# Where the operands of the matrix products lie in SBUF: moved by part of 512 bytes, by role

## The chip, the core and the metric

The kernel runs on one core of a Trainium2 chip. The metric is the device time of one execution in microseconds (us). TensorE (PE) multiplies a stationary operand, loaded beforehand by a weight load (PEld), with a moving operand that streams through it; VectorE (DVE), ScalarE (ACT) and GpSimd (POOL) work on tiles in SBUF, and SyncE (SP) and GpSimd issue DMAs. SBUF has 128 partitions; a tile takes the same byte range in each, and an address below is the byte in a partition.

## What is computed

Two layers of an encoder on 512 tokens of 1024 features, in float32. Layer 0 mixes tokens by neighbourhood attention on an 8 x 64 grid, layer 1 by three dilated windowed attentions that are merged by their softmax denominators. Each layer ends in a gated feed-forward part with 2816 hidden features.

```
for layer in range(2):
    h = rms_norm(x, norm_mix_pre[layer])
    h = neighbourhood_attention(h, ...) if layer == 0 else dilated_attention(h, ...)
    x = x + rms_norm(h, norm_mix_post[layer])
    h = rms_norm(x, norm_ffn_pre[layer])
    x = x + rms_norm(swiglu(h, w_gate, w_up, w_down), norm_ffn_post[layer])
swiglu(x) = (silu(x @ w_gate) * (x @ w_up)) @ w_down
```

## The kernel before

**How a product is made.** Each float32 operand is split into a high part `h` and a low part `l`, both in float32r, by ACT (line 365) and DVE (line 366). `mm3` (lines 377 to 379) makes one product as three matmuls: h by h, h by l, l by h. In its calls `s` is stationary (128 columns are loaded as weights) and `m` is moving (256 or 512 columns). A trace row such as `gu<-rxa,h_c` names the output in PSUM, then both operands; in these rows the moving operand stands first, except that one name stands alone when both lie in the same tile.

**Seven products for eight.** A unit of class `Seven` makes a 2 by 2 block product with seven products of 12 `mm3` matmuls each (84 in all), from sums of weights and sums of activations: p1, p2, d1, s2, s4, s3, x2b. Gate and up of one block of 128 hidden features make one unit, so `gate_up` runs 22 units a layer (output `gu`), with the first products of three units ahead. Query and key of a pair of heads make one unit too: 8 in layer 0 (output `pp_n`), 24 in layer 1 (`pp_d`). `Values` does the same for the values of layer 1 (`vd`), with the activations stationary and the weights moving. In all of these the moving operand has 256 columns.

**Where the operands lie.** The ring of weights is the pool `wpool`: eight tiles `h_*` and `l_*` of 4096 bytes, turned over by the split. Activations lie in `rxa` (ten parts of D = 1024), `rxc` (five parts and a bit) and `rxb` (an arena that is opened for the mixers). The weights of the product s4 go to a ring of two slots: `vmem` and the last part of `rxc` (layer 0's mixer: the last part of `ao`). So in gate/up the moving operands are X1A and X1B in `rxc` and D1, S2, S4, S3, X2B in `rxa`; in the mixers X1A, X1B, X2B and D1 are in `rxa` and S2, S4, S3 in `rxb`.

**512 columns.** `down` turns the roles round: the hidden activations are split into a ring `hl_` of five parts of `rxc` and are stationary, the weights from the ring `wpool` are moving with 512 columns (outputs `yd_s`, `yd_pp`). `out_proj` (output `yo`) has the attention's result in `rxa` stationary and moves the output weights, which are split into two ring tiles, `wm` and `vmem`, the last part of `rxa`, and `rxb`.

**Order.** Class `Order` simulates the instructions on five engines with fixed costs and pins each engine's order. Its costs do not depend on SBUF addresses, but which instruction waits for which does depend on what overlaps in a tile.

**Places.** The allocator puts the tiles of `cpool` one behind the other, then `wpool`, then the arenas. Parts are whole multiples of 512 bytes, so every operand of a tile has its tile's residue modulo 512, but for score operands with an extra 64 columns (256 bytes).

Of the kernel before, what the change touches and what calls it, by code (L numbers as in the profile page):

```python
# [13 lines left out]
F32 = mybir.dt.float32  # L14
F32R = mybir.dt.float32r
# [15 lines left out]
EPS = 1e-6  # L31
MEM, ARENA = 14544, 9 * D
NEG = -1e30
BIG = 3.0e38
X1A, X1B, X2B, D1, S2, S4, S3 = range(7)
BANKS = {"pp": 3, "s": 2, "t": 2, "o": 1}
SLOPES = [float(np.float32(2.0) ** np.float32(-8.0 * (h + 1) / HEADS)) for h in range(HEADS)]
# [259 lines left out]
def encoder_kernel(ctx: ExitStack, tc: tile.TileContext, a: dict, out: bass.AP):  # L297
# [3 lines left out]
    cpool = ctx.enter_context(tc.tile_pool(name="cpool", bufs=1))  # L301
    wpool = ctx.enter_context(tc.tile_pool(name="wpool", bufs=4))
    psum = ctx.enter_context(tc.tile_pool(name="psum", bufs=1, space=bass.MemoryType.PSUM))
    dpool = ctx.enter_context(tc.tile_pool(name="dpool", bufs=1, space=bass.MemoryType.DRAM))

    ident = cpool.tile([P, P], F32, name="ident")
    make_identity(nc, ident)
    mhalf = cpool.tile([P, 1], F32, name="mhalf")
    dve.memset(mhalf, -0.5)
    spill = [dpool.tile([NT, P, D], F32, name=f"spill{i}") for i in range(3)]  # L310
# [12 lines left out]
    rxa = cpool.tile([P, 10 * D], F32R, name="rxa")  # L323
    rxc = cpool.tile([P, 5 * D + 256], F32R, name="rxc")
    vmem = cpool.tile([P, D], F32R, name="vmem")

    mem = cpool.tile([P, MEM], F32, name="mem")
    rvd = [dpool.tile([PAIRS, P, D], F32, name=f"rvd{i}") for i in range(2)]
# [18 lines left out]
    def w22_ring(mem):  # L347
        return cycle([hl(vmem, 0, 512), hl(mem, 0, 512)])

    small_ = cycle(range(20))  # L350

    def small(name, n=1):
        if "o0" in name or "o1" in name:
            return tagged(cpool, [P, n], F32, f"small_o{next(small_)}", name, 1)
        return tagged(cpool, [P, n], F32, f"small{n}", name, 16 if n > 1 else 12)
# [463 lines left out]
    def gate_up(layer, xs, hid, more, rings, sums):  # L819
        wg, wu = a["wg"], a["wu"]  # L820
        raws = ring(more, 0, 2 * D, 3)
        g_, u_, p5_ = rings
        v_ = w22_ring(rxc[:, 4 * D:5 * D])
        units, us = {}, {}
# [186 lines left out]
    def hl(mem, i, n):  # L1011
        return mem[:, i * D:i * D + n], mem[:, i * D + n:i * D + 2 * n]
# [24 lines left out]
    def mix_out(layer, w, rxb, wm, load_x):  # L1037
        for j in range(PAIRS - 1):
            nc.gpsimd.dma_start(rxa[:, j * D:(j + 1) * D], rvd[layer][j])

        us = [None] * 2 + [hl(wm, 0, D), (wm[:, 2 * D:], vmem), hl(rxa, 8, D)] + [hl(rxb, 2 * i, D) for i in range(3)]

        out_proj(w, rv, layer, load_x, us, (ring(mem, 4 * D, D, 4), ring(mem, 0, D, 4), ring(mem, 13440, 512, 2)),
                 (mem[:, 11392:11392 + D], mem[:, 12416:12416 + D]))

    def ffn(layer, stack, memc):
        hl_ = ring(rxc, 0, D, 5)
        rxb = None
# [98 lines left out]
    inner.close()  # L1147
    with arena("wm0", 3 * D, "right", F32R) as wm:
        mix_out(0, a["na_o"], rxb, wm, lambda xt, t: nc.sync.dma_start(xt, a["x_rows"][t]))
# [13 lines left out]
    p5_ = ring(memc, 2560, 256, 2)  # L1163
    q_, k_, kl_, ost_ = rxc[:, 0:D], rxc[:, D:2 * D], rxc[:, 2 * D:3 * D], ring(rxc, 3 * D, D, 1)
    w22_ = w22_ring(rxc[:, 4 * D:5 * D])
    def by_token(v):
# [192 lines left out]

    vus, vslots = {}, cycle([hl(rxc, 0, D), hl(rxc, 2, D), (vmem, rxc[:, 4 * D:5 * D])])  # L1360
    for qd in range(2):
# [67 lines left out]
    inner.close()  # L1429
    with arena("wm1", 3 * D, "right", F32R) as wm:  # L1430
        mix_out(1, a["dil_o"], rxb, wm, load_block)
# [92 lines left out]
```

## Time and profile before

| | us |
|---|---|
| three runs: median (lowest to highest) | 1484.54 (1484.52 to 1489.98) |
| the profiled execution | 1487.69 |
| its span, from the first to the last instruction | 1485.9 |

A window of the trace gives the busy time of each engine in a stretch of the span. The stages lie about so (us from the span's start): layer 0's mixer to 205, its output projection to 264, gate/up to 490, down to 597; layer 1's values to 735, its queries, keys and attention to 1070, the output projection to 1144, gate/up to 1376, down to 1478. Matmuls overlap in the pipeline, and the duration of one is modelled; the distance from one start to the next is measured, and is what to read of a stream of them. A weight load starts some 3 ns behind the matmul ahead of its own.

### The profile page before, as it was taken

How to read it: one execution, taken by the hardware profiler on the slowest of the kernel's cores; microseconds unless marked ns; L12 is line 12 of the kernel's file. 1: busy time of each engine (PE TensorE's matmuls, PEld its weight loads, DVE VectorE, ACT ScalarE, POOL GpSimd, SP SyncE). 2: the span in 40 equal slices, each digit the busy share in tenths (PEclk: the TensorE clock that was granted, in tenths of full speed). 3: DMA queues.
4: the chain of work that ended last, by engine and by line, in shares of the span. 5: the costliest groups of instructions: out<-in, count | busy, mean ns of one | idle time of the engine just before them, and what ended most of it. 6: DMA issues, size and time to landing. Idle time of an engine off the chain costs nothing.

```text
span 1485.9 us, 27934 instructions
## 1 busy us (share of the span) xinstructions
PE 1442.8 (97%) x10788; PEld 1333.1 (90%) x10788; DVE 1196.8 (81%) x1876; ACT 904.1 (61%) x1819; POOL 542.4 (37%) x398
## 2 busy tenths in 40 slices
PE   7999999899999999999999999999999999999997
PEld 6988877899999888899999999989977999999886
DVE  5499967699889788797689788787657989998877
ACT  4478874555555567544467778876675654555664
POOL 5345425544231001665555444334204644330001
PEclk9999999899999999999999999999999999999999
DMA  5346487677333664435433343333766788834662
GB/s 200 139 177 179 155 286 206 227 221 212 114 112 114 204 220 162 168 126 187 142 100 101 93 145 116 100 133 103 237 206 214 200 243 243 252 126 149 203 208 92
DMA packets 86645, 253.22 MB, mean 170 GB/s; under 512 B 19312, under 2 KB 31600, under 8 KB 84464
## 3 DMA queue, kind: packets, MB, share of 16 engines
q1 hardware_dynamic: 77696, 197.69, 40.4%
q0 software_dynamic: 8672, 53.48, 13.9%
q8 instruction: 85, 1.39, 0.4%
q14 instruction: 48, 0.39, 0.1%
q10 hardware_dynamic: 144, 0.26, 0.0%
HBM read 229.24 MB, written 68.29 MB: 200 GB/s over the span
## 4 chain that ended last, share of the span: by engine, by line
PE 77%; DVE 8%; ACT 7%; DMA 3%; issue 3%; POOL 1%; SPq 0%; POOLq 0%; DVEq 0%; ACTq 0%
PE gu L377 10%; PE gu L378 9%; PE gu L379 9%; PE pp_d L377 5%; PE pp_d L379 4%; PE pp_d L378 4%; PE yd_s L377 3%; PE yd_s L379 3%; PE yd_s L378 3%; PE yd_pp L377 2%; PE yd_pp L379 2%; PE yd_pp L378 2%; PE sb L1274 2%; PE yo L377 2%; PE yo L379 1%
## 5 line engine op out<-in xcount | busy, mean ns | idle before, releaser
L585 POOL TENSOR_TENSOR rs_yd<-v_yd,mhalf 128x1 f32<-128x1 f32 x8 | 8.3, 1043 | 261.3 <-DVE v_yd L583 261.3
L378 PE MATMUL gu<-rxa,h_b 128*128 128x256 f32 x352 | 100.0, 284 | 2.5 <-DVE rxa L602 2.5
L377 PE MATMUL gu<-rxc,h_a 128*128 128x256 f32 x352 | 99.7, 285 | 2.0 <-ACT h_a L365 1.2
L377 PE MATMUL gu<-rxa,h_c 128*128 128x256 f32 x352 | 99.7, 283 | 1.3 <-DVE memc L839 1.1
L378 PE MATMUL gu<-rxc,h_a 128*128 128x256 f32 x352 | 99.7, 284 | 1.2 <-DVE rxc L602 1.0
L377 PE MATMUL gu<-rxa,h_b 128*128 128x256 f32 x352 | 99.7, 284 | 1.2 <-ACT rxa L601 1.2
L379 PE MATMUL gu<-rxa,l_b 128*128 128x256 f32 x352 | 99.6, 283 | 0.2 <-DVE l_b L366 0.2
L379 PE MATMUL gu<-rxc,l_a 128*128 128x256 f32 x352 | 99.1, 282 | 0.0
L378 PE MATMUL gu<-rxa,h_c 128*128 128x256 f32 x352 | 98.7, 280 | 0.0
L379 PE MATMUL gu<-rxa,l_c 128*128 128x256 f32 x352 | 98.3, 280 | 0.0
L365 ACT ACTIVATE rxc<-mem 128x512 fp32r<-128x512 f32 (+2 forms) x90 | 55.9, 624 | 65.9 <-PE yd_pp L378 33.8
L445 POOL TENSOR_TENSOR r_d<-r_d 128x512 f32<-128x512 f32 x24 | 36.1, 1506 | 161.0 <-DVE l_ad L366 122.9
L445 POOL TENSOR_TENSOR r_gu<-r_gu 128x512 f32<-128x512 f32 x20 | 30.6, 1529 | 149.8 <-DVE l_a L366 102.4
L366 DVE TENSOR_TENSOR rxc<-mem,rxc 128x512 fp32r<-128x512 f32 (+2 forms) x90 | 64.4, 719 | 19.5 <-ACT rxc L365 19.2
L445 POOL TENSOR_TENSOR raw<-raw 128x512 f32<-128x512 f32 x24 | 38.0, 1582 | 99.4 <-DVE l_a L366 74.7
L378 PEld LDWEIGHTS gu<-rxa,h_b 128*128 128x128 f32 x352 | 67.6, 192 | 2.7 <-DVE rxa L602 2.7
L377 PEld LDWEIGHTS gu<-rxc,h_a 128*128 128x128 f32 x352 | 67.1, 192 | 2.8 <-ACT h_a L365 1.4
L377 PEld LDWEIGHTS gu<-rxa,h_c 128*128 128x128 f32 x352 | 66.5, 189 | 2.9 <-DVE memc L839 1.3
L378 PEld LDWEIGHTS gu<-rxc,h_a 128*128 128x128 f32 x352 | 67.2, 191 | 1.8 <-DVE rxc L602 1.8
L377 PEld LDWEIGHTS gu<-rxa,h_b 128*128 128x128 f32 x352 | 67.3, 192 | 1.5 <-ACT rxa L601 1.4
L1238 ACT ACTIVATE mem<-mem 128x256 f32<-128x256 f32 x128 | 63.8, 504 | 7.5 <-DVE mem L1237 7.3
L379 PEld LDWEIGHTS gu<-rxa,l_b 128*128 128x128 f32 x352 | 67.4, 191 | 0.4 <-DVE l_b L366 0.4
(610 smaller groups left out, 6157.7 us busy)
## 6 DMA issues: line engine op xcount, KB each, us to landing
wsum<-wd POOLq DMA_DIRECT2D x24, 1408.0 KB, 12.1
r_d<-dil_qk SPq DMA_DIRECT2D x48, 512.0 KB, 4.1
raw<-wg SPq DMA_DIRECT2D x24, 512.0 KB, 5.1
raw<-wu SPq DMA_DIRECT2D x24, 512.0 KB, 8.4
wsum<-wsum POOLq DMA_DIRECT2D x8, 1408.0 KB, 10.3
raw<-wsum SPq DMA_DIRECT2D x22, 512.0 KB, 4.3
r_gu<-wg SPq DMA_DIRECT2D x20, 512.0 KB, 3.8
r_gu<-wu SPq DMA_DIRECT2D x20, 512.0 KB, 4.9
```

Of the source, the lines that this page charges most:

```text
L365: act.activation(h, src, AF.Copy)
L366: dve.tensor_sub(l, src, h.bitcast(F32))
L377: i = pe.matmul(o, s[0], m[0], start=start, stop=False, skip_group_check=True)
L378: pe.matmul(o, s[0], m[1], start=False, stop=False, skip_group_check=True)
L379: pe.matmul(o, s[1], m[0], start=False, stop=stop, skip_group_check=True)
L445: self.added = e[0].tensor_add(q[0], q[0], q[2])
L585: pool.tensor_tensor(r, v, mhalf, op=ALU.pow)
L1238: act.activation(pr[:, f], pr[:, f], AF.Exp, bias=st[:, c:c + 1], scale=-1.0, accum_out=st[:, c + 2:c + 3])
L1274: pe.matmul(ss[hd][:, f0:f0 + P], qf[rw, block(c)], kf[rw, block(c)], start=True, stop=True)
```

## The change

It shifts tiles so that residues modulo 512 differ or agree by role. `ident` and `mhalf` change places, `mem` comes ahead of `vmem`, the twenty small tiles `small_o*` become columns of one tile `few_small`, a pad of 48 floats ends the last pool ahead of the arenas, `wm` is 80 floats longer, and five parts of `rxc` are taken from 80 floats (320 bytes) on, as `rxs`: the `hl_` ring of `down`, the s4 slot, and in layer 1 the keys, the result's ring and the slots of `Values`. X1A and X1B of gate/up and the queries stay at `rxc`'s start. `rxb`, which is allocated behind the pad, starts at another residue.

In the built programs the residues are:

| tile | before | after |
|---|---|---|
| `rxa`, `rxc`, `mem` | 160 | 160 |
| `rxs`, the shifted parts of `rxc` | 160 (unshifted) | 480 |
| `vmem` | 160 | 480 |
| ring of weights `h_*`, `l_*` | 480 | 480 |
| `rxb`, the weights' raw arena | 480 | 160 |
| `wm` | 480 | 160 |
| `memc`, `akl`, `ao` | 480 | 480 |
| `ident` | 128 | 160 |

Of the 8,056 float32r matmuls with 256 moving columns, 1,760 have both operands at one residue before and 48 after; of the 1,308 with 512 columns, 64 before and 1,196 after.

No instruction is added or removed. The order is the same on all engines but at the end of layer 0's gate/up and the start of its down, where the first parts of the `hl_` ring now overlap two of gate/up's operands in `rxc`. On DVE, there, the low parts of down's first activations (`rxc<-mem`) and those of the last units' weights (`l_b`, `l_c`; `r_gu` and `raw` are weights as loaded) stood before as:

```order
L366 TENSOR_TENSOR rxc<-mem,rxc 128x512
L366 TENSOR_TENSOR l_b_19_5179<-raw_2880,h_b_19_5178 128x1024
L841 TENSOR_TENSOR memc_2876<-mem,gu_18_4749 128x256
L366 TENSOR_TENSOR l_c_19_5238<-raw_2880,h_c_19_5237 128x1024
L845 TENSOR_TENSOR mem<-memc_2876,mem 128x2x256
L366 TENSOR_TENSOR l_b_20_5260<-r_gu_20_4977,h_b_20_5259 128x1024
L836 TENSOR_TENSOR memc_2876<-memc_2876,gu_21_5096 128x256
L366 TENSOR_TENSOR l_c_20_5319<-r_gu_20_4977,h_c_20_5318 128x1024
L435 MEMSET gu_21_5096 128x256
L845 TENSOR_TENSOR mem<-memc_2876 128x2x256
L366 TENSOR_TENSOR rxc<-mem,rxc 128x512 x3
```

and stand now as:

```order
L373 TENSOR_TENSOR l_b_19_5156<-raw_2857,h_b_19_5155 128x1024
L852 TENSOR_TENSOR mem<-memc_2853,mem 128x2x256
L848 TENSOR_TENSOR memc_2853<-mem,gu_18_4726 128x256
L373 TENSOR_TENSOR l_c_19_5215<-raw_2857,h_c_19_5214 128x1024
L373 TENSOR_TENSOR rxc<-mem,rxc 128x512 x2
L373 TENSOR_TENSOR l_b_20_5237<-r_gu_20_4954,h_b_20_5236 128x1024
L843 TENSOR_TENSOR memc_2853<-memc_2853,gu_21_5073 128x256
L373 TENSOR_TENSOR l_c_20_5296<-r_gu_20_4954,h_c_20_5295 128x1024
L442 MEMSET gu_21_5073 128x256
L852 TENSOR_TENSOR mem<-memc_2853 128x2x256
L373 TENSOR_TENSOR rxc<-mem,rxc 128x512
```

One split of down's activations stood ahead of the four splits of gate/up's weights, and three behind them; now two stand in their middle, and the next ones behind. On PE, at the same place, the products of units 20 and 21 (`gu_20`, `gu_21`) and the first of down (`yd_pp`) stood before as:

```order
L379 MATMUL gu_20_4980<-rxa,l_c_20_5319 128x256
L377 MATMUL gu_20_4980<-rxa,h_c_20_5318 128x256
L378 MATMUL gu_20_4980<-rxa,h_c_20_5318 128x256
L379 MATMUL gu_20_4980<-rxa,l_c_20_5319 128x256
L377 MATMUL gu_21_5096<-rxa,rxc 128x256
L378 MATMUL gu_21_5096<-rxa,rxc 128x256
L379 MATMUL gu_21_5096<-rxa,rxc 128x256
L377 MATMUL gu_21_5096<-rxa,rxc 128x256
```

and stand now as:

```order
L385 MATMUL gu_20_4957<-rxa,h_c_20_5295 128x256
L386 MATMUL gu_20_4957<-rxa,l_c_20_5296 128x256
L385 MATMUL gu_21_5073<-rxa,h_b_21_5317 128x256
L386 MATMUL gu_21_5073<-rxa,l_b_21_5318 128x256
L384 MATMUL yd_pp_5410<-h_d0p_0_5415,rxc 128x512
L385 MATMUL yd_pp_5410<-l_d0p_0_5416,rxc 128x512
L384 MATMUL gu_20_4957<-rxa,h_c_20_5295 128x256
L385 MATMUL gu_20_4957<-rxa,h_c_20_5295 128x256
```

Between two dozens of matmuls of unit 20 stood six of unit 21's s4; now two of its product before and two of down's first stand there, and the six come later. Names end in running numbers, which differ in the two programs by a constant.

The diff:

```diff
@@ -29,10 +29,11 @@
 COLS = 64
 ROWS = 8
 EPS = 1e-6
-MEM, ARENA = 14544, 9 * D
+MEM, ARENA = 14544, 9 * D + 80
 NEG = -1e30
 BIG = 3.0e38
 X1A, X1B, X2B, D1, S2, S4, S3 = range(7)
+SHIFT = 80
 BANKS = {"pp": 3, "s": 2, "t": 2, "o": 1}
 SLOPES = [float(np.float32(2.0) ** np.float32(-8.0 * (h + 1) / HEADS)) for h in range(HEADS)]
 
@@ -300,13 +301,13 @@
 
     cpool = ctx.enter_context(tc.tile_pool(name="cpool", bufs=1))
     wpool = ctx.enter_context(tc.tile_pool(name="wpool", bufs=4))
+    zpool = ctx.enter_context(tc.tile_pool(name="zpool", bufs=1))
     psum = ctx.enter_context(tc.tile_pool(name="psum", bufs=1, space=bass.MemoryType.PSUM))
     dpool = ctx.enter_context(tc.tile_pool(name="dpool", bufs=1, space=bass.MemoryType.DRAM))
 
+    mhalf = cpool.tile([P, 1], F32, name="mhalf")
     ident = cpool.tile([P, P], F32, name="ident")
     make_identity(nc, ident)
-    mhalf = cpool.tile([P, 1], F32, name="mhalf")
-    dve.memset(mhalf, -0.5)
     spill = [dpool.tile([NT, P, D], F32, name=f"spill{i}") for i in range(3)]
 
     tags, arenas, extra = {}, [], []
@@ -322,9 +323,15 @@
 
     rxa = cpool.tile([P, 10 * D], F32R, name="rxa")
     rxc = cpool.tile([P, 5 * D + 256], F32R, name="rxc")
+
+    mem = cpool.tile([P, MEM], F32, name="mem")
     vmem = cpool.tile([P, D], F32R, name="vmem")
 
-    mem = cpool.tile([P, MEM], F32, name="mem")
+    few_small = cpool.tile([P, 32], F32, name="few_small")
+    pad = zpool.tile([P, 48], F32, name="pad")
+    dve.memset(mhalf, -0.5)
+
+    rxs = rxc[:, SHIFT:SHIFT + 5 * D]
     rvd = [dpool.tile([PAIRS, P, D], F32, name=f"rvd{i}") for i in range(2)]
 
     tops = {"left": 0, "right": 0}
@@ -347,11 +354,11 @@
     def w22_ring(mem):
         return cycle([hl(vmem, 0, 512), hl(mem, 0, 512)])
 
-    small_ = cycle(range(20))
+    small_ = cycle([few_small[:, i:i + 1] for i in range(20)])
 
     def small(name, n=1):
         if "o0" in name or "o1" in name:
-            return tagged(cpool, [P, n], F32, f"small_o{next(small_)}", name, 1)
+            return next(small_)
         return tagged(cpool, [P, n], F32, f"small{n}", name, 16 if n > 1 else 12)
 
     def load2(srcs, name, raw=None):
@@ -820,7 +827,7 @@
         wg, wu = a["wg"], a["wu"]
         raws = ring(more, 0, 2 * D, 3)
         g_, u_, p5_ = rings
-        v_ = w22_ring(rxc[:, 4 * D:5 * D])
+        v_ = w22_ring(rxs[:, 4 * D:])
         units, us = {}, {}
 
         def unit_of(f):
@@ -1038,13 +1045,13 @@
         for j in range(PAIRS - 1):
             nc.gpsimd.dma_start(rxa[:, j * D:(j + 1) * D], rvd[layer][j])
 
-        us = [None] * 2 + [hl(wm, 0, D), (wm[:, 2 * D:], vmem), hl(rxa, 8, D)] + [hl(rxb, 2 * i, D) for i in range(3)]
+        us = [None] * 2 + [hl(wm, 0, D), (wm[:, 2 * D:3 * D], vmem), hl(rxa, 8, D)] + [hl(rxb, 2 * i, D) for i in range(3)]
 
         out_proj(w, rv, layer, load_x, us, (ring(mem, 4 * D, D, 4), ring(mem, 0, D, 4), ring(mem, 13440, 512, 2)),
                  (mem[:, 11392:11392 + D], mem[:, 12416:12416 + D]))
 
     def ffn(layer, stack, memc):
-        hl_ = ring(rxc, 0, D, 5)
+        hl_ = ring(rxs, 0, D, 5)
         rxb = None
         hm = mem[:, :FT * 512]
         h2 = hm.rearrange("p (h x) -> p h x", h=2)
@@ -1145,7 +1152,7 @@
              lambda v: v.rearrange("p (i c) -> p i c", i=ROWS))
 
     inner.close()
-    with arena("wm0", 3 * D, "right", F32R) as wm:
+    with arena("wm0", 3 * D + 80, "right", F32R) as wm:
         mix_out(0, a["na_o"], rxb, wm, lambda xt, t: nc.sync.dma_start(xt, a["x_rows"][t]))
     stack.close()
     memc = inner.enter_context(arena("memc0", 3 * D, "right"))
@@ -1161,8 +1168,8 @@
     pt_, few_ = ring(ap, 10 * D, D, 4), ring(mem, 0, 96, 2)
     bt, qs, ks = memc[:, 0:1536].rearrange("p (k c) -> p k c", c=P), memc[:, 1536:2048], memc[:, 2048:2560]
     p5_ = ring(memc, 2560, 256, 2)
-    q_, k_, kl_, ost_ = rxc[:, 0:D], rxc[:, D:2 * D], rxc[:, 2 * D:3 * D], ring(rxc, 3 * D, D, 1)
-    w22_ = w22_ring(rxc[:, 4 * D:5 * D])
+    q_, k_, kl_, ost_ = rxc[:, 0:D], rxs[:, D:2 * D], rxs[:, 2 * D:3 * D], ring(rxs, 3 * D, D, 1)
+    w22_ = w22_ring(rxs[:, 4 * D:])
     def by_token(v):
 
         return v.rearrange("p (m r) -> p r m", r=4)
@@ -1357,7 +1364,7 @@
     order = [3 * j + g for j in range(PAIRS) for g in orders[j]]
     stats, parts, weight, pts, vg, ready, left, later = {}, {}, {}, {}, {}, [], {}, {}
 
-    vus, vslots = {}, cycle([hl(rxc, 0, D), hl(rxc, 2, D), (vmem, rxc[:, 4 * D:5 * D])])
+    vus, vslots = {}, cycle([hl(rxs, 0, D), hl(rxs, 2, D), (vmem, rxs[:, 4 * D:])])
     for qd in range(2):
         v = v_quarter(ap[:, (6 + qd) * D:(7 + qd) * D], a["dil_v"][0, qd], f"d{qd}")
         nc.sync.dma_start(vd[0][qd].rearrange("t p c -> p t c"), v)
@@ -1427,7 +1434,7 @@
                 nc.sync.dma_start(xt[32 * r + 16:32 * r + 32], rows[r, 0:16])
 
     inner.close()
-    with arena("wm1", 3 * D, "right", F32R) as wm:
+    with arena("wm1", 3 * D + 80, "right", F32R) as wm:
         mix_out(1, a["dil_o"], rxb, wm, load_block)
     stack.close()
     memc = inner.enter_context(arena("memc1", 3 * D, "right"))
```

## The prediction

> **What bounds the kernel now.** I read the page first, then windows by stage, then the timeline of TensorE alone. The page:
>
> ```profile
> span 1485.9 us, 27934 instructions
> ...
> PE 1442.8 (97%) x10788; PEld 1333.1 (90%) x10788; DVE 1196.8 (81%) x1876; ACT 904.1 (61%) x1819; POOL 542.4 (37%) x398
> ...
> PE 77%; DVE 8%; ACT 7%; DMA 3%; issue 3%; POOL 1%; SPq 0%; POOLq 0%; DVEq 0%; ACTq 0%
> ```
>
> TensorE makes 77% of the chain that ended last. The windows (stretch and its length; busy time and count of PE, PEld, DVE, ACT, POOL; granted clock; DMA share; GB/s) say where it never rests:
>
> ```profile
> 300.00:425.00 125.00, 125.00 (x1063) 125.00 (x1062) 114.75 (x138) 65.64 (x113) 48.62 (x32) 1.00 0.60 176
> 490.00:597.00 107.00, 107.00 (x483) 88.31 (x482) 92.44 (x124) 68.93 (x108) 7.00 (x4) 1.00 0.61 197
> 735.00:1070.00 335.00, 330.77 (x2837) 310.45 (x2837) 262.62 (x551) 243.65 (x619) 141.30 (x93) 1.00 0.40 122
> 1175.00:1345.00 170.00, 168.69 (x1427) 168.06 (x1426) 155.43 (x189) 87.23 (x152) 66.62 (x45) 1.00 0.76 214
> 1376.00:1478.00 102.00, 101.74 (x437) 82.06 (x435) 82.79 (x112) 61.38 (x96) 3.02 (x3) 1.00 0.54 171
> ```
>
> Gate/up (rows 1 and 4) and down (rows 2 and 5) have PE busy for nearly all their length at a granted clock of 1.00: there the time is the number of matmuls times the distance from one start to the next. Gate/up is 1063 in 125.00 us (117.6 ns each) and 1427 in 168.69 us (118.2 ns). So the question is whether places change that distance. The timeline has starts to 10 ns, so I divide long runs (first column start, second modelled duration):
>
> ```profile
> 299.78 0.28 PE L378 MATMUL gu<-rxa,h_c 128*128 128x256 f32 x1
> ...
> 305.11 0.28 PE L378 MATMUL gu<-rxc,h_a 128*128 128x256 f32 x1
> 305.22 0.28 PE L377 MATMUL gu<-rxa,vmem 128*128 128x256 f32 x1
> ...
> 306.54 0.28 PE L379 MATMUL gu<-rxa,vmem 128*128 128x256 f32 x1
> 306.65 0.28 PE L379 MATMUL gu<-rxc,l_a 128*128 128x256 f32 x1
> ...
> 312.66 0.28 PE L379 MATMUL gu<-rxc,l_a 128*128 128x256 f32 x1
> ```
>
> This is the key view. From 299.78 to 305.11 lie 47 steps: 113.4 ns each; moving operand at 160 modulo 512 bytes, weights from the ring at 480. From 305.22 to 306.54, 11 steps with weights in vmem at 160, the same residue as the moving operand: 120.0 ns. From 306.65 to 312.66 the weights are in the ring again, yet 51 steps take 117.8 ns each. So there are **three paces of 256 columns**: 120 when the places agree, and for places apart a fast one (113.4) and a slow one (117.8). Before the agreeing run the pace is fast, behind it slow, and it stays slow through the rest of the stretch. Is it the place, or vmem?
>
> ```profile
> 737.72 0.28 PE L378 MATMUL pp_d<-rxb,vmem 128*128 128x256 f32 x1
> ...
> 738.89 0.28 PE L379 MATMUL pp_d<-rxb,vmem 128*128 128x256 f32 x1
> 742.66 0.28 PE L378 MATMUL pp_d<-rxb,h_cd 128*128 128x256 f32 x1
> ...
> 743.38 0.28 PE L378 MATMUL pp_d<-rxb,h_cd 128*128 128x256 f32 x1
> ```
>
> With the moving operand in rxb at 480, vmem is apart: 10 steps in 1.17 us, 117. And there the ring, itself at 480, gives 120 (6 steps in 0.72). The place it is.
>
> **The change part by part.** It adds no instruction and removes none but names; all it does to the time must come through these paces, or through waits.
>
> ```profile
> L378 PE MATMUL gu<-rxa,h_b 128*128 128x256 f32 x352 | 100.0, 284 | 2.5 <-DVE rxa L602 2.5
> L378 PE MATMUL gu<-rxa,vmem 128*128 128x256 f32 x88 | 24.9, 283 | 0.0
> L377 PE MATMUL pp_d<-rxb,h_cd 128*128 128x256 f32 x96 | 27.8, 290 | 0.7 <-DVE mem L683 0.7
> ```
>
> *Gate/up, 256 columns.* 9 groups like the first row (x352) and 6 like the second (x88) are 3,696 matmuls, 528 of them on agreeing places, one group of 12 in each unit of 84. After the change all are apart. Direct gain: 528 x (120.0 - 117.8) = 1.2 us. The larger one: nothing throws the fast pace out any more. If all of the 1063 + 1427 ran at 113.4, that is 125.00 + 168.69 - 2490 x 0.1134 = 11.3 us; the other 1,206, in stretches broken by waits and partly fast already, I put at 2 us: at most 13.3. Not all will be fast, since a wait can end in either pace:
>
> ```profile
> 1347.76 0.39 PE L377 MATMUL gu<-rxa,h_c 128*128 128x256 f32 x1
> 1347.99 0.28 PE L378 MATMUL gu<-rxa,h_c 128*128 128x256 f32 x1
> ...
> 1349.04 0.28 PE L378 MATMUL gu<-rxa,h_c 128*128 128x256 f32 x1
> ```
>
> Here a disturbed start (one step of about 0.23 us) is followed by 9 steps in 1.05 us, 117: slow, with no agreeing place near; the stretch above at 299.78 came out of its wait fast. Of the 50 stretches of eight steps or more that begin behind a wait with these two residues, the first at 80 us and the last at 1372, the timeline has 34 at the fast pace. I take three quarters, since the one at 299.78 would have run on for a third of the layer. A quarter at the slow pace gives back 0.25 x 3,696 x 4.4 ns = 4.1 us: **-9.3 us**, bounds 0 (all slow) and -13.3.
>
> What hides it: DVE is busy 114.75 of 125.00 us in the first row of windows. At the fast pace that stretch lasts 120.5; DVE would fill 95% of it. It still fits, barely, which is a reason not to count on all of it.
>
> *Query/key products of both mixers.* 6 groups like the third row have rxb against the ring, 576 agreeing, and layer 0's 8 units 24 each the same way, with 48 more in ao; afterwards apart. 816 x (120 - 115, between both paces) = 4.1 us, but PE has gaps there (330.77 of 335) and transposes and scores disturb it in every unit: I keep half, **-2.0**, bounds 0 and -5.
>
> *Value products and scores of layer 1.* Here the change makes moving 480, stationary 160, apart the other way round. The nearest rows, vmem above at 117, have that order at the slow pace. 5 units of 7 products of 24 matmuls are 840, over half of them apart already: **+0.5**, bounds -2 and +2.
>
> *Down and output projection, 512 columns.* Down was apart (160 and 480) and becomes equal:
>
> ```profile
> 521.55 0.39 PE L377 MATMUL yd_pp<-h_d0d,rxc 128*128 128x512 f32 x1
> ...
> 577.86 0.39 PE L377 MATMUL yd_s<-h_d0s,rxc 128*128 128x512 f32 x1
> 1400.58 0.40 PE L377 MATMUL yd_pp<-h_d1d,rxc 128*128 128x512 f32 x1
> ...
> 1457.98 0.40 PE L377 MATMUL yd_s<-h_d1s,rxc 128*128 128x512 f32 x1
> 227.78 0.39 PE L377 MATMUL yo<-rxa 128*128 128x512 f32 x1
> 228.46 0.63 PE L377 MATMUL yo<-rxb,rxa 128*128 128x512 f32 x2
> 248.88 0.40 PE L377 MATMUL yo<-rxa 128*128 128x512 f32 x1
> ...
> 250.27 0.40 PE L377 MATMUL yo<-rxb,rxa 128*128 128x512 f32 x1
> ```
>
> 246 steps each: 228.9 ns in layer 0, 233.3 in layer 1: two paces again, for one and the same code. Equal places exist before only in yo with both operands in rxa: 3 steps in 0.68 us, 226.7, the shortest seen; another such group has 6 in 1.39, 231.7. Two of the eight short groups reach 226.7. Over 924 matmuls of down that is -4.1 us if both layers catch the short pace, +0.5 if neither does. By the count of groups I take **-1.0**; yo's own 224 that become equal stand beside waits: 0, bounds +-1.
>
> *The rest.* small_o values in one tile: the same instructions wait for the same engines; 0. Transposes keep their form with ident 32 bytes further; the nearest price is the 6.6 ns between agreeing and fast at 256 columns, on some 340: 0, bounds 0 and +2. The moved order at the end of layer 0's gate/up is one slot of operands later on DVE, where PE sat busy from 425 on; 0, bounds +-1.
>
> Sum: -9.3 - 2.0 + 0.5 - 1.0 = **-11.8 us**. The profiled execution took 1487.69 us (span 1485.9 and 1.8 around it), so 1475.9 in its place. It is 3.15 over the median of the three runs (1484.54), of which layer 1's slow pace in down may be 437 x 4.4 ns = 1.9 us; from the median the sum gives 1472.7.
>
> A rule speaks against the change: the Trainium skill, "TensorE: Matmul & The Clock Gate", section "Step-by-step: what each phase is for", says that TensorE has two independent read ports and that loading the next weights takes no read bandwidth from the running matmul. By it places would be without effect. The rows at 305.22 and 742.66 disagree, at 120.0 against 113.4. The same page, "Wait — 56ns, not 53.3ns?", puts a step at columns over 2.4 GHz plus about 2.5 ns, an estimate of 109.2 for 256; no steady stretch here is below 113.
>
> **The rivals.**
> 1. *The slow pace sticks.* Every stretch of gate/up drops to 117.8 whatever the places. For it: long stretches are slow now, and the wait at 1347.76 ends slow. Against: 47 steps at 113.4 without a break. Time: the direct gains alone, -1.2 and some -1 in the mixers, and +0.5 for the values: about 1483.
> 2. *Places have no effect*, and the paces come from tiles or the state of the engine: 1484.5. Against it the two views of vmem.
> 3. *DVE becomes the bound of gate/up, and it gets slower than before.* The place is the splits of weights beside GpSimd's sums. DVE has 125.00 - 114.75 = 10.3 us free over some 12.6 units, 0.8 us a unit. A faster PE shifts which sums meet on their shared SBUF path; from 0.8 us more collision a unit on, PE waits in every unit, and each such wait may drop the pace too. At 1 us more a unit, 44 units x 0.2 = 9 us: 1493. Against it: no instruction is added, and the wait would hold PE back again, which undoes the shift.
> 4. *All goes fast*, gate/up whole and down at 226.7: -13.3 - 4.1 - 2.0 + 0.5 = -18.9: 1465.6.
>
> **How the numbers follow.** Forecast 0.50; rival 4 0.17; rival 1 0.20; rival 2 0.08; rival 3 0.05. Half a per cent, about what a measurement of this kernel can tell from no change, is 7.4 us: below 1477.1 counts as faster. Forecast (mostly) and rival 4 are faster: 0.67. Rivals 1, 2 and a little of the forecast are within: 0.29. Rival 3: 0.04. The range from 1464 to 1484 leaves out about half of rivals 2 and 4, and rival 3.
>
> **What would show it.** Gate/up's x84 a unit in 9.5 us instead of 9.9; no 120 ns stretch behind vmem or rxc; whole units at 113 between waits; the two downs at one of 226.7 or about 231. Wrong would be: gate/up at 117.8 throughout (rival 1), waits for DVE before gu in every unit (rival 3), down above 233.

## The result, and the profile after

| | before | after |
|---|---|---|
| time, us, median (range) of 7 runs each, beside each other | 1489.98 (1484.52 to 1493.61) | 1478.99 (1475.11 to 1480.66) |
| profiled execution, us | 1487.69 | 1480.66 |
| ratio of times | 1 | 0.9933, 95% interval 0.9915 to 0.9950 |

The kernel became faster by 0.67%, beyond the half per cent that can be told from no change. The seven runs of before have a higher median than the three shown ahead of the prediction. From the page of the changed kernel, the span, the busy times and the engines of the chain that ended last:

```profile
span 1478.8 us, 27934 instructions
...
PE 1433.6 (97%) x10788; PEld 1326.6 (90%) x10788; DVE 1200.2 (81%) x1876; ACT 904.0 (61%) x1819; POOL 542.5 (37%) x398
...
PE 76%; DVE 11%; ACT 7%; issue 2%; DMA 2%; POOL 1%; SPq 0%; POOLq 0%; DVEq 0%; ACTq 0%
```

The same instructions, 9.2 us less of busy PE; DVE's part in the chain went from 8% to 11%. The windows of gate/up in layer 0, of layer 1's mixer and of gate/up in layer 1 (columns as before):

```profile
300.00:425.00 125.00, 125.00 (x1063) 124.89 (x1061) 114.98 (x139) 66.96 (x115) 48.26 (x33) 1.00 0.62 180
...
735.00:1070.00 335.00, 328.73 (x2839) 307.51 (x2838) 266.81 (x559) 247.00 (x627) 139.02 (x94) 1.00 0.40 124
1175.00:1345.00 170.00, 168.46 (x1430) 167.84 (x1429) 156.47 (x191) 89.06 (x155) 66.35 (x45) 1.00 0.74 208
```

The first row had 1063 matmuls before, too, and the last 1427 where 1430 stand now: in the middle of gate/up, where the forecast had its largest term, next to nothing was won. TensorE's timeline there (start, modelled duration):

```profile
302.72 0.28 PE L384 MATMUL gu<-rxa,vmem 128*128 128x256 f32 x1
...
304.02 0.28 PE L386 MATMUL gu<-rxa,vmem 128*128 128x256 f32 x1
304.14 0.28 PE L386 MATMUL gu<-rxc,l_a 128*128 128x256 f32 x1
...
310.03 0.28 PE L385 MATMUL gu<-rxc,h_a 128*128 128x256 f32 x1
310.26 0.32 PE L384 MATMUL gu<-rxa,rxc 128*128 128x256 f32 x1
310.42 0.28 PE L385 MATMUL gu<-rxa,rxc 128*128 128x256 f32 x1
...
424.77 0.28 PE L384 MATMUL gu<-rxa,h_b 128*128 128x256 f32 x1
```

The weights in vmem no longer step at 120.0: 11 steps in 1.30 us, 118.2, and the 50 behind them, from 304.14 to 310.03, 117.8. No agreeing place is near, and yet the pace is the slow one, and it stays: from 310.42 to 424.77 lie 971 steps of 117.8 ns without one wait. Down, the same 246 steps in each layer as before:

```profile
501.58 0.39 PE L384 MATMUL yd_pp<-h_d0p,rxc 128*128 128x512 f32 x1
...
557.34 0.39 PE L384 MATMUL yd_s<-h_d0s,rxc 128*128 128x512 f32 x1
1379.37 0.39 PE L384 MATMUL yd_pp<-h_d1p,rxc 128*128 128x512 f32 x1
...
1435.13 0.39 PE L384 MATMUL yd_s<-h_d1s,rxc 128*128 128x512 f32 x1
```

55.76 us both times, 226.7 ns a step, where 228.9 and 233.3 stood.

For what follows, each kernel's timeline of TensorE was added up by stage: a stage is the sum of the distances from each of its matmuls to the next start. In gate/up (3,696 matmuls in two layers) a distance of 135 ns or more is called a wait, with its excess over 113.3; the others are steps. A step made while the clock was granted at half takes 213 ns and so falls among the waits: such steps are 3.8 us of the waits before and 3.1 after, all of them in the first 40 us of layer 0's gate/up (granted clock 0.87 before and 0.91 after in the window 257:297).

| gate/up, profiled executions | steps at 115 ns or less, layer 0 / 1 | mean step, ns | waits, excess us, both layers | both layers, us |
|---|---|---|---|---|
| before | 224 / 251 | 117.5 / 117.4 | 16.2 | 450.0 |
| after | 516 / 438 | 116.5 / 116.7 | 16.3 | 447.1 |

By the same sums the query/key products went from 339.5 to 338.3 us, layer 1's value products from 101.9 to 102.0, down from 213.4 to 209.5.

**The theories.** A: the distance of the weights from the moving operand, modulo 512, sets which paces are possible; among those a wait draws one, and it lasts to the next wait. At the fast pace PE catches up with DVE, waits and draws again, while a slow PE waits for nothing: slow lasts. B: the paces are luck, or the work of other engines. C came up on the way: at the fast pace DVE is the bound.

### The profile page after: what moved, and what is told of

It reads as the page before. It is cut to its first block, busy times and chain, and to the rows that moved or that the text cites. A ratio compares the mean times of both kernels' runs of the same rounds, so it can differ in the third digit from the quotient of the medians.

```text
span 1478.8 us, 27934 instructions
## 1 busy us (share of the span) xinstructions
PE 1433.6 (97%) x10788; PEld 1326.6 (90%) x10788; DVE 1200.2 (81%) x1876; ACT 904.0 (61%) x1819; POOL 542.5 (37%) x398
## 4 chain that ended last, share of the span: by engine, by line
PE 76%; DVE 11%; ACT 7%; issue 2%; DMA 2%; POOL 1%; SPq 0%; POOLq 0%; DVEq 0%; ACTq 0%
PE gu L384 9%; PE gu L385 9%; PE gu L386 9%; PE pp_d L384 4%; PE pp_d L386 4%; PE pp_d L385 4%; PE yd_s L384 3%; PE yd_s L385 3%; PE yd_s L386 3%; PE yd_pp L384 2%; PE yd_pp L385 2%; PE yd_pp L386 2%; PE vd L385 2%; PE vd L384 2%; PE vd L386 2%
## 5 line engine op out<-in xcount | busy, mean ns | idle before, releaser
L452 POOL TENSOR_TENSOR r_gu<-r_gu 128x512 f32<-128x512 f32 x20 | 30.3, 1516 | 150.1 <-DVE l_a L373 116.7
```

Source lines behind the costliest of these rows:

```text
L452: self.added = e[0].tensor_add(q[0], q[0], q[2])
```

## The experiments

**One part alone.** Four kernels ran beside each other. First, the kernel before with down's half of the change:

```diff
-        hl_ = ring(rxc, 0, D, 5)
+        hl_ = ring(rxc, 80, D, 5)
```

> The kernel before with one part of the change alone: down's weights 320 bytes further, so that its 512 columns and their weights agree modulo 512 bytes; nothing else moves. Theory A (places set the paces, and each stretch drifts into the pace of its places): both downs step at about 226.9 ns as in the changed kernel (104.9 and 104.6 us against 105.9 and 107.5), everything else as before; 1 to 4 us less than the kernel before, ratio 0.997 to 0.999. Theory B (the paces are luck, drawn anew at each wait or each execution): down at 229 or 233 in one of the layers as before, ratio 1.000 within 0.001.

Measured: ratio 0.9973 (0.9962 to 0.9984), 1484.43 us median. The new order of PE at the end of layer 0's gate/up comes with this half; the next run has the old one. Down 105.0 and 104.6 us, steps of 227.0 and 226.8. As A has it: down is worth 0.27%, 4.0 us of 1488.64. Gate/up, whose operands lie as before, had 554 steps at the fast pace and took 446.5 us, 3.5 less than in the execution of before and even less than the changed kernel's 447.1. So two executions differ in gate/up by as much as the 2.9 us of the pair above.

Second, the changed kernel without that half:

```diff
-        hl_ = ring(rxs, 0, D, 5)
+        hl_ = ring(rxc, 0, D, 5)
```

> The changed kernel with down put back to places that are apart; the part for 256 columns stays. Theory A: gate/up and the products of the mixers as in the changed kernel (gate/up 225.6 and 221.5 us), down back at 229 to 233 ns; 2 to 5 us less than the kernel before, ratio 0.9965 to 0.9985. Theory B: as likely over as under the kernel before, by the pace that the long stretches of gate/up catch. If the two parts add, this run and the one with down alone make up together what the change made (ratio 0.9933).

Measured: 0.9961 (0.9945 to 0.9976); down back at 229.2 and 233.3. The two parts add: 0.9973 x 0.9961 is 0.9934, the change made 0.9933. All that isn't down is worth 5.8 us of 1488.64 by this ratio. The ratio is a little better than A's numbers, and the profile says why: this execution drew the fast pace oftener, 1,109 and 1,013 of the 1,848 steps a layer. And it shows what such a draw meets. TensorE's timeline of this run:

```profile
362.45 0.28 PE L386 MATMUL gu<-rxa,l_b 128*128 128x256 f32 x1
362.56 0.28 PE L384 MATMUL gu<-rxa,h_b 128*128 128x256 f32 x1
363.41 0.39 PE L384 MATMUL gu<-rxa,h_c 128*128 128x256 f32 x1 [0.57 <-DVE memc L846]
363.63 0.28 PE L385 MATMUL gu<-rxa,h_c 128*128 128x256 f32 x1
...
423.11 0.28 PE L384 MATMUL gu<-rxa,h_b 128*128 128x256 f32 x1
```

Up to 362.56 PE stepped at 113.3; then it waits 0.57 us for DVE's subtraction in L846, which reads the bank to which the next product adds. In the slow execution above PE passed this place without a wait. Behind it come 505 steps of 117.8, from 363.63 to 423.11. So here the pace was lost to a wait that the slow pace didn't have.

**DVE relieved.** Third and fourth, in the changed kernel and in the one before, one of DVE's sums in each unit of gate/up is shortened. It is made on 32 of its 512 columns, so these kernels leave out part of what is computed; the planner still reckons with 512, and the order stays:

```diff
-            e[2].tensor_add(q[3], q[0], q[3])
+            c = 32 if e[2] is dve else 512
+            e[2].tensor_add(q[3][:, :c], q[0][:, :c], q[3][:, :c])
...
```

> The changed kernel, but in each unit of gate/up DVE's sum of 512 columns (0.88 to 1.07 us in the changed profile, 43.3 us in 44 units) is made on 32 columns only; the order of every engine is unchanged, and part of the reference's sum is left out. Theory A (at the fast pace PE runs into DVE's results, has a short wait, draws a new pace there, and a slow draw lasts because a slow PE waits for nothing): with 0.9 us a unit less on DVE the fast stretches of gate/up last longer than some 40 steps and most of its 3,696 steps are at 113.3 ns; gate/up falls from 447 us to 425 to 437, so 10 to 20 us less than the changed kernel, ratio to the kernel before 0.98 to 0.987. Theory B (a draw at each wait, DVE without part in it): still mostly 117.8 or as it falls out, ratio 0.991 to 0.996 as the changed kernel.

Measured: 0.9909 (0.9891 to 0.9926). Short of A's numbers and at the edge of B's: the fast pace came in one layer only. Layer 0 had 1,604 of 1,848 steps at the fast pace and took 218.7 us in place of 225.6; layer 1 drew slow ahead of its longest stretch and had 394 (223.2 us). The long stretch of layer 0 in this run:

```profile
308.82 0.28 PE L387 MATMUL gu<-rxa,rxc 128*128 128x256 f32 x1
...
418.87 0.28 PE L386 MATMUL gu<-rxa,h_b 128*128 128x256 f32 x1
```

It is the same 971 steps that took 114.35 us in the changed kernel, here 110.05 us, 113.3 each, with no wait among them. So the fast pace lasted here with DVE relieved, where it broke off in the run above; relief doesn't call it, though. The draw stays.

> The kernel before with the same sum on 32 columns, order unchanged, part of the reference's sum left out. Theory A: the run of 12 on agreeing places in each unit still ends the fast pace, so PE is at 117.8 to 120 ns for most of each unit whatever DVE does: under 3 us less than the kernel before, ratio 0.998 to 1.000; with the changed kernel's version of this run it shows that places decide once DVE gives room. If instead DVE is what holds gate/up in both kernels, this run gains as much as that of the changed kernel (10 us or more).

Measured: 0.9989 (0.9976 to 1.0002), gate/up 451.7 us, 413 fast steps. The same relief is worth nothing measurable ahead of the change: there the agreeing run in each unit ends the fast pace, not DVE.

**The matmuls alone.** The next three are no encoders but streams of matmuls in the pattern of the products, so that places can be tried that the kernel hasn't got:

```python
...
s = [sta[:, shift + j * 1024 + k * P:shift + j * 1024 + k * P + P] for j in range(2)]
m = [mov[:, j * 2048 + k * n:j * 2048 + k * n + n] for j in range(2)]
for x, y in ((0, 0), (0, 1), (1, 0)):
    chain(pe.matmul(o, s[x], m[y], ...))
...
```

> Not the kernel but its matmuls alone: streams of 48 steps of 256 columns and 24 of 512 in the pattern of the products (two weights, two moving operands, three matmuls), each stream behind a wait for DVE to read its bank, weights 0 to 480 bytes (modulo 512, in steps of 32) behind the moving operands, each of the 16 distances eight times; DVE, ACT and GpSimd otherwise idle, the reference isn't computed. Theory A (the distance modulo 512 sets which paces are possible, the wait draws among them): distance 0 steps at 120.0 ns (256 columns) and 226.7 (512) in all eight; the changed kernel's distance (weights 320 bytes behind the moving operand) at 113.3 in about 70% of the eight and 117.8 in the rest; the opposite one (192 behind) mostly 117.8; within a stream the pace doesn't change after some six steps. Theory B (the paces come from the work of the other engines, or from the state of the chip): with all others idle every distance steps alike, or the pace differs from one repetition of the same distance to the next as much as between distances. If some distance steps at 113.3 in all eight, it would be a better place for 256 columns than the one of the changed kernel.

Measured, mean of the second half of each stream, 256 columns: distance 0 at 120.0 (but for the very first stream of all, 140.7); 64 at 113.3 four times and 117.8 four times; 320 at 113.3 seven times of eight; 192 at 117.8 eight times, 448 seven; 160, 256 and 416 at 120.0 like 0; the rest between 116.7 and 118.8. For 512 columns 0 and 256 at 226.7, 192 and 448 at 228.9, all else 231.7 to 234.6. With every other engine idle the paces are those of the kernel, and they go with the distance: B falls as far as the paces go. The pattern repeats after 256 bytes, not 512. And no common distance of both weights is fast in every stream, so the distance of the change is the best of the sixteen and still a draw.

In the grid the low half of the weights is shifted apart from the high half.

> Matmuls of 256 columns alone again, streams of 36 steps behind a wait. First, distances (weights behind the moving operands, modulo 512) of 296 to 344 bytes around the changed kernel's 320, eight times each; then the two weights' distances apart from each other, each of 256 to 480 bytes in steps of 32, four times each. If the fast pace of 113.3 ns needs the one distance of 320 exactly for both weights (theory A with a narrow window), only 320/320 shows it, in about 70% of its streams, and every other pair lies between 115 and 120. If one of the two weights alone decides (the one whose distance to the running operand enters twice in each three matmuls), the rows of 320 for it show 113.3 whatever the other is. If a pair shows 113.3 in all four, a place exists from which gate/up would not draw at all, and the kernel can be built on it. If nothing differs beyond what one stream differs from the next (theory B), the distances of the run before were chance.

Measured: of 64 pairs two were at 113.3 in all four streams, high half 320 and low 448 bytes behind the moving operand, and the reverse; 320/320 itself four times at 117.8. Around 320 the window is narrow: 312 to 328 are at 117.4 to 120.2; 344 had 113.3 to 113.4 in six of eight and 116.6 in two.

> Matmuls alone, longer streams (60 steps of 256 columns sixteen times, 36 of 512 eight times), the wait ahead of each of eight lengths, so that one and the same distance is entered in different ways. The grid left two pairs, weights 320 and 448 bytes (high and low halves) behind the moving operands or the other way round, at 113.3 in all eight of their streams. Theory A with a lock (such a pair lets the streams fall into the fast pace whatever the wait was): 320/448 and 448/320, and 64/192 and 192/64 since the distances repeat after 256 bytes, at 113.3 in 14 or more of 16; 320/320 at 113.3 in 8 to 14 and at 117.8 in the rest; the opposite direction (192/192) at 117.8 in at least 13; 0/0 at 120.0 in all. Theory B (the grid's eight were chance, 70% each, which happens once in 17 times): the pairs draw like 320/320, 8 to 14 of 16. Two more forms move the low half of the moving operand instead of that of the weights; if it is the distance within each matmul's own pair that counts, 320/320 with the low moving half 128 bytes ahead locks too. For 512 columns: both operands equal 226.7 in all; low halves both 128 bytes further the same; only one of them further between 226.7 and 233.3.

Measured: 320/448 at 113.3 in 16 of 16, 64/192 in 16 of 16; 192/64 in 13; 448/320, against the expectation and the grid's four of four, in 1 of 16, the others at 118.9. 320/320 in 7 or 8 of 16 (the first only towards its end), 192/192 at 117.8 in 15, 0/0 at 120.0 in all. Moving the low half of the moving operand doesn't lock (117.8 in all 16). For 512 columns 0/0 has 226.7; with a low half moved, of one operand or of both, 231.1 to 233.3, where equal shifts of both were expected to be free. Rows of whole streams (start, us for 60 matmuls, wait ahead): 0/0, a 320/320 that drew slow, then one that drew fast, 320/448, 448/320, 64/192 and 192/192:

```profile
90.44 7.46 PE L54 MATMUL b<-mov,sta 128*128 128x256 f32 x60 [0.51 <-DVE res L58]
98.40 7.33 PE L54 MATMUL b<-mov,sta 128*128 128x256 f32 x60 [0.51 <-DVE res L58]
...
555.51 7.08 PE L54 MATMUL b<-mov,sta 128*128 128x256 f32 x60 [0.77 <-DVE res L58]
563.44 7.08 PE L54 MATMUL b<-mov,sta 128*128 128x256 f32 x60 [0.84 <-DVE res L58]
571.36 7.40 PE L54 MATMUL b<-mov,sta 128*128 128x256 f32 x60 [0.84 <-DVE res L58]
579.60 7.10 PE L54 MATMUL b<-mov,sta 128*128 128x256 f32 x60 [0.84 <-DVE res L58]
...
611.81 7.34 PE L54 MATMUL b<-mov,sta 128*128 128x256 f32 x60 [0.84 <-DVE res L58]
```

7.33 and 7.08 at one and the same distance are the draw. It isn't mere chance here: of the fifteen streams of 320/320 behind the first, the seven that follow a stream of 512 columns are all slow, and of the eight that follow 256 columns seven are fast. So in 14 of these 15 the pace went with what came before the stream, or with the length of its wait, which alternated with it: the run doesn't part the two.

**The lock in the kernel.** 320/448 takes the draw away, so it tells what the fast pace is worth. For it the low halves of the weights were put in one tile, with slots 128 bytes further for the products of 256 columns; of s4's weights all high halves went to `vmem` and all low halves to `rxs`, 128 bytes further too. First comes the control with no shift, then the shift, then the shift with DVE relieved. The main lines of the edit:

```diff
...
-        return tuple(tagged(wpool, [P, D], F32R, f"w{i}", f"{i}_{name}", 4) for i in "hl")
...
+        c = (0, 3, 2, 1)[len(names) % 4] * D + apart
...
+        return h, lows[0][:, c:c + D]
...
```

> The changed kernel with the low halves of the weights in one tile of four slots rather than in four tiles, all operands at the residues of the changed kernel; the planner's order comes out a little different from it. It is the control for the next run. Theory A: gate/up draws its pace at waits as in the changed kernel, mean step of the matmuls without a wait 115 to 117 ns; time within 0.5% of the changed kernel, ratio to the kernel before 0.989 to 0.998.

> The same with the low halves of the weights 128 bytes further for the products of 256 columns (weights 320 and 448 bytes behind the moving operand, the pair that took every stream of the matmuls alone to 113.3 ns); down and output projection keep their places. Theory A with a lock: no stretch of gate/up or of the query/key products stays at 117.8, mean step without a wait 113.3 to 114 there; that is 2.5 to 3 ns on some 3,550 + 2,450 steps, 15 to 18 us, of which gate/up gives back what it waits for DVE at that pace (in the run that had half its steps fast, waits took 3.4 us of the gain in layer 1): 5 to 12 us less than the control, ratio to the kernel before 0.984 to 0.990. Theory B (in the kernel the other engines set the pace, what the matmuls show alone doesn't carry over): steps as in the control, time as the control within 0.2%. Theory C (DVE is the bound of gate/up): steps at 113.3, but gate/up's 447 us stay within 3 us and PE's waits for DVE grow by as much as the steps save; then only the query/key products gain, 3 to 5 us.

> The run with the lock, and DVE's sum of 512 columns in each unit of gate/up made on 32 only, same order, part of the reference's sum left out. If DVE takes back the gain of the lock in gate/up (theory C, and in part A), this run is 5 to 12 us below the one with the lock, more than the 4.5 us that the same relief gave the changed kernel, with gate/up near 1,848 x 113.4 ns = 210 us a layer and its waits. If DVE has no part in it, under 3 us below.

Measured: control 0.9944 (0.9929 to 0.9959); lock 1.0009 (0.9992 to 1.0026); lock and relief 0.9970 (0.9952 to 0.9988). The lock did what the matmuls alone had shown, 1,630 and 1,568 fast steps (control 1,165 and 949), mean 113.8 and 113.9, and yet the kernel was slower than the control by 10 us, which none of the theories had. The planner had come out with another order for the lock than for the control. Gate/up's waits in excess were 22.4 us in the control, 39.8 with the lock and 22.3 with relief in the lock's own order. These executions overstate what relief does: that of the lock was the slowest of its twelve (1496.85 us), that with relief the second fastest of its own (1478.57); the medians differ by 6.4 us. PE's largest waits in gate/up of layer 0 with the lock (sum, times, longest):

```profile
PE gu L403 <- DVE mem L867: 6.1, 1, 6.1
PE gu L403 <- ACT rxc L627: 2.0, 1, 2.0
```

One wait for DVE of 6.1 us has no like in the other runs. The trace tells what stood ahead of it (rows of DVE and GpSimd, in order of time):

```profile
306.86 1.21 DVE L384 TENSOR_TENSOR wl<-raw,h_c 128x1024 fp32r<-128x1024 f32 x1
...
312.18 1.28 POOL L471 TENSOR_TENSOR r_gu<-r_gu 128x512 f32<-128x512 f32 x1 [23.38 <-DMA r_gu<-wu]
...
316.20 6.65 DVE L384 TENSOR_TENSOR wl<-raw,h_c 128x1024 fp32r<-128x1024 f32 x1
...
316.42 1.71 POOL L471 TENSOR_TENSOR r_gu<-r_gu 128x512 f32<-128x512 f32 x1
...
320.09 1.67 POOL L472 TENSOR_TENSOR raw<-raw 128x512 f32<-128x512 f32 x1
```

GpSimd had waited 23.4 us for a load of weights, and of its sums behind that four stand one behind the other, from 316.42 to about 321.8. DVE's split beside them took 6.65 us, where the same kind of split had taken 1.21 shortly before. With relief, in the same order, GpSimd has a like wait (20.2 us), but no split on DVE between 306 and 323 us takes over 1.7 us. So the 6.1 us came with a meeting of DVE and GpSimd in this execution, and nothing shows that the pace brought it.

The clock granted to TensorE has a part too: it is 0.992 on average over the lock's twelve runs and 0.997 over the control's six. As time not granted, (1 - clock) times the time, that is 11.6 against 4.7 us, so 6.9 of the 10 us, an estimate that holds if TensorE was the bound all the time. In the profiled execution of the lock steps at half the clock are 10.4 of the 39.8 us of waits, in the control 2.9 of the 22.4. What the pace is worth, and how much of it DVE takes back, can't be told from these three. So the last two keep the order: the low halves of all weights in the rings 128 bytes further by a gap between the tiles (and a pad smaller by as much), which moves no instruction. s4's weights stay at 320/320.

```diff
...
-        return tuple(tagged(wpool, [P, D], F32R, f"w{i}", f"{i}_{name}", 4) for i in "hl")
+        h = tagged(wpool, [P, D], F32R, "wh", f"h_{name}", 4)
+        if not gaps:
+            gaps.append(wpool.tile([P, 32], F32, name="gap", bufs=1))
+        return h, tagged(wpool, [P, D], F32R, "wl", f"l_{name}", 4)
...
```

> The changed kernel with the order of every engine unchanged and the low halves of all weights in the rings 128 bytes further (in gate/up three of four products at 320 and 448 bytes behind the moving operand, the fourth still at 320 and 320). The order of the run with the lock before had come out differently and had waits of its own (one of 6.1 us for DVE); here that is excluded. Down pays, since its weights' low halves move away from the place that agrees: 231.1 in place of 226.9 ns a step, 3.9 us in both layers by the matmuls alone. Theory A (the pace was what cost): steps of gate/up without a wait 113.4 to 114.2 in place of 116.6, 8 to 11 us less there, of which DVE may take a third; with 3.9 us back in down and 1 to 3 us won in the query/key products 2 to 9 us less than the changed kernel, ratio to the kernel before 0.987 to 0.992. Theory C (at the fast pace DVE is the bound): steps at 113.4 to 114.2, PE's waits in gate/up grow by about what the steps save, the two layers stay within 2 us of 225.6 and 221.5; with down's 3.9 us the run is 0 to 4 us above the changed kernel, ratio 0.993 to 0.997.

> The same with DVE's sum of 512 columns in each unit of gate/up made on 32 columns, order unchanged, part of the reference's sum left out. If theory C holds, DVE's 0.9 us a unit sets the gain free: gate/up at 1,848 x 113.5 ns = 210 us and some 8 us of waits a layer, so 216 to 220 in both layers; 5 to 12 us below the run without the relief. If the waits are for something else, less than 3 us below it.

Measured: lock 0.9929 (0.9916 to 0.9942), 1477.17 us median; with relief 0.9904 (0.9886 to 0.9922), 1474.03 us. The lock's ratio lies between A's numbers and C's.

| gate/up, same order | steps at 115 ns or less, layer 0 / 1 | mean step, ns | waits, excess us | both layers, us |
|---|---|---|---|---|
| changed kernel | 516 / 438 | 116.5 / 116.7 | 16.3 | 447.1 |
| and relief | 1604 / 394 | 113.9 / 116.9 | 15.6 | 441.9 |
| and lock | 1623 / 1583 | 113.8 / 114.0 | 21.2 | 442.1 |
| and lock, relief | 1682 / 1623 | 113.7 / 113.9 | 14.3 | 434.9 |

Of the excess of the steps over 113.3, 12.0 us in the changed kernel, the lock leaves 2.2. It saves 9.9 us in steps and gives 4.9 back as waits; with relief the waits are 6.9 us less. Not all of that is DVE's. Beyond the first 40 us of gate/up in each layer the waits are 5.8 us in the changed kernel, 9.0 with the lock and 4.8 with relief: there the lock gives back 3.2 us, a third of what its steps save, and relief frees them. The rest of the differences, 1.7 and 2.7 us, lies in those first 40 us, where the granted clock of the three executions was 0.91, 0.87 and 0.96 in layer 0 (window 257:297). The medians put relief at 3.1 us, with intervals that overlap; its profiled execution, 1469.46 us, is 4.6 below its median. The windows of the run with the lock, the same stretches as above:

```profile
300.00:425.00 125.00, 124.11 (x1090) 123.70 (x1089) 118.49 (x143) 67.51 (x117) 50.34 (x33) 1.00 0.60 180
1175.00:1345.00 170.00, 168.22 (x1457) 166.53 (x1456) 160.36 (x196) 90.63 (x159) 66.64 (x45) 1.00 0.74 214
```

27 matmuls more in each, and DVE at 118.49 of 125 us, 95%, where it was 92%. One group of each kernel from the view that groups instructions by line and tile (busy, mean ns, idle before and what ended it), names DVE's reads of the bank again. The changed kernel:

```profile
L384 PE MATMUL gu<-rxa,h_c 128*128 128x256 f32 x352 | 99.9, 284 | 2.0 <-DVE memc L846 1.3 <-DVE mem L846 0.3 <-DVE memc L848 0.3
```

The run with the lock, where L846 and L848 have become L851 and L853:

```profile
L389 PE MATMUL gu<-rxa,h_c 128*128 128x256 f32 x352 | 99.4, 283 | 2.8 <-DVE memc L851 1.2 <-DVE memc L853 1.2 <-DVE mem L851 0.2
```

So A and C both have a part: the pace costs, and DVE takes some of it back, about a third by one execution of each. The query/key products won 1.1 us. Down lost 2.9 us (212.4 us) by the shift of its low halves, so the whole is not to be told from the changed kernel: 0.9929 and 0.9933 with intervals that overlap. No run found an order-keeping version that beats the changed kernel beyond doubt and computes all of it.

## Why the prediction was right, and where it was not

The forecast was 1472.7, -11.8 us; the medians of seven differ by 11.0, the profiled pair by 7.0, and by the ratio it is 10.0. 6.3 us lie between forecast and measured median, and a good part is the base: the three runs that it was taken from had a median of 1484.54, the 23 of the first and of the second later comparison 1488.64 and 1488.80. By its steps:

- *Places set the paces*: right, and shown twice, by each half of the change alone and by the matmuls alone. The Trainium skill, "TensorE: Matmul & The Clock Gate", section "Step-by-step: what each phase is for", which makes the two reads independent, doesn't hold for this pattern: 120.0 against 113.3 ns with all other engines idle (rival 2). The modulus is 256 rather than 512, which changes nothing for the change's own places.
- *Gate/up -9.3, "three quarters at the fast pace"*: this is the step that failed. The profiled pair shows -2.9, with 954 fast steps of 3,696, a quarter. Single executions differ by as much, so the better measure is the change without down's half: 5.8 us for gate/up, query/key and values together, where the forecast had 10.8. The count of stretches carried over well (80 of 112 behind a wait were fast afterwards, 71%; 34 of 50 before), but stretches were counted, not their steps: at the fast pace PE can run into DVE, and then the stretch is short, while the slow one lasted for 971 steps. The 971 steps were fast in one profiled run (with relief), slow in the changed kernel's, and fast, then slow for 505 steps, in the one without down's half.
- *"It still fits, barely"*: DVE at 95% was forecast and is what the lock shows, 118.49 of 125 us. It doesn't quite fit: about a third of what the steps save comes back as waits. Rival 3 named the right engine; its price was too high in the kernel's own order, where gate/up still gained 5.0 us, and a long meeting of sums such as it feared, with a split of 6.65 us, is seen in the lock's other order.
- *Query/key -2.0*: -1.2 in the profiled pair; the steps gave some 4 us, as reckoned, and 3 came back as waits. *Values +0.5*: +0.1; the steps went from 116.0 to 117.3 ns, to the slow pace as reckoned. Both within their bounds.
- *Down -1.0, by the count of eight short groups*: mis-sized; it is -3.9, close to the best bound, -4.1. Equal places have one pace for 512 columns: all eight streams alone at 226.7, both layers at 226.9 on average, and 0.27% by itself. The short groups of the output projection, of six steps at most in the rows shown, were the wrong row to count: alone, the second to the twelfth step of 512 columns at a distance of 256 average 227.5 to 232.1 ns, and the last twelve 226.7.

So two sizes were off in opposite directions and in part made up for each other: that the forecast's -11.8 came so near the medians' -11.0 is in part luck. The sum of the stages, -2.9 - 1.2 + 0.1 - 3.9 = -7.9, answers to the pair's -7.0.

What stays open: what at the end of a wait decides the draw; what the waits for DVE cost over many executions, since each kernel has one profile and the granted clock differs between them; and how far each of seven runs was fast, since only profiled executions show paces.

## What to carry to other kernels

Where matmuls stand start to start, divide long runs of starts in the timeline by their count: a step that differs between two runs of the same shape can be a place, not work, and it adds up: 4.5 ns on gate/up's 3,696 steps are 17 us, over one per cent. Weigh such paces by steps, not by stretches, and ask how long a state lasts once it is drawn. Before counting the whole gain of a faster engine, look at the next one: DVE, 92% busy, took back about a third. And before comparing the waits of two executions, compare their granted clocks.

## What the hardware showed that was not expected

- The pace of a stream depends on the distance of weights and moving operand modulo 256 bytes, and on that of the low and high halves of the weights: 320/448 always ended at 113.3 (16 of 16, and four of four in the grid), 448/320 in 1 of 16, but in four of four in the grid, behind other streams.
- Of the sixteen common distances, 256 columns are fastest at 64 bytes modulo 256 (113.3 in 11 of 16 streams, 117.8 in the rest) and slowest at 0 and 160 (120.0), 512 columns fastest at 0 (226.7): a place that serves both doesn't exist among those tried.
- One and the same pattern keeps one of two paces for as long as nothing disturbs it (971 steps at 113.3 in one execution, at 117.8 in another), and in the streams alone the way in went with it: behind a stream of 512 columns all seven of 320/320 were slow, behind 256 columns seven of eight fast.
- A split of 128x1024 on DVE took 6.65 us beside four sums of GpSimd made one behind the other, where it took 1.21 us shortly before.
